# S5 scan chain in two PSUM banks of the product's ring, its steps spread over the whole first product

## The chip, the core and the metric

The kernel runs on one core of a Trainium2 chip, as one program. The metric is the device time of one execution in microseconds (us); lower is better. The engines are called as in the profile: PE (TensorE matmul), DVE (VectorE), ACT (ScalarE), POOL (GpSimd) and SP (SyncE, which here only starts DMAs). SBUF is the working memory of all engines; PSUM is the memory of eight banks that PE writes its results to, and that DVE and ACT can read and write.

## The reference

The whole reference is an S5 layer, an attention layer and a mixed attention and RWKV layer, on 512 positions of 2048 channels. The change lies in the first product of the S5 layer and in the scan beside it; the rest of the program stays as it is.

```python
def s5_ssm(u, a_re, a_im, log_dt, b_re, b_im, c_re, c_im, d_skip):
    """u: (B,S,W) -> Re(C h_t) + D*u_t, h_t = Abar h_{t-1} + Bbar u_t per 16-channel group."""
...
    _, _, h_re, h_im = lax.associative_scan(combine, (a_seq_re, a_seq_im, x_re, x_im), axis=1)
    y = (jnp.einsum('bsgp,gcp->bsgc', h_re, c_re.astype(F32))
         - jnp.einsum('bsgp,gcp->bsgc', h_im, c_im.astype(F32)))
...
def s5_layer(h, g_pre, g_post, w_in, ...):
    xn = rmsnorm(h, g_pre)
    uz = xn @ w_in
    u, z = jnp.split(uz, 2, axis=-1)
    y = s5_ssm(u, a_re, a_im, log_dt, b_re, b_im, c_re, c_im, d_skip)
    y = jax.nn.gelu(y)
    y = y * jax.nn.sigmoid(y @ w_glu.astype(F32) + b_glu.astype(F32))
    y = y.astype(h.dtype) * jax.nn.silu(z)
    return h + rmsnorm(y @ w_out, g_post)
```

## The kernel before, in words

**The first product.** `phase1` computes `xn @ w_in` as 32 tiles of 128 channels by 512 positions, 16 for u and 16 for z, in the order `order1`: five z tiles first (`ZF`), then a u tile every 1.35 tiles (`UR`), and z tiles between and behind them. A tile (`gemm`) is four chunks of 12 matmuls of 128x512, into one bank `acc` of the ring `pq`, which has four PSUM banks. Each chunk calls `tick` once, so the program counts 128 ticks in this product. Its weights come as `raw` by DMA; ACT rounds them to `wh` (L199), and DVE subtracts to get the rest `wl` (L200, both inputs in SBUF). PE can't begin a chunk without its `wh` and `wl`.

**The scan beside it.** The 128 groups of the S5 layer are done in 16 steps j of eight groups. POOL makes the matrices `In` and `Ox` of four groups at a time (`s5_pool`, 32 calls of six operations, L505 to L507) from the power tables `PT` and `Q` and the inputs `bc`. PE makes from them `kb` and the transposes `tb` (`s5_mats`), and ACT copies these out. A finished u tile is scaled on DVE, goes to DRAM (`ud`) and comes back in another order (`U`), and PE multiplies `InT` with `U` into the bank `xb` (`s5_x`). Then comes the chain of the step on DVE: the rotation (`s5_rot`, L609 to L612), the scan along time (`s5_scan`, L618), ACT's copies with halves exchanged (`Gw`), and the rotation back into `H` (`s5_back`, L630 to L632). PE then computes `yb` (`s5_y`, L642 without H, L644 with H), and DVE and ACT apply the gelu (`s5_gelu`, `s5_out`, L652 and L658), whose result goes to DRAM as `y2d`. `s5_phase` makes the rotation tables (L574 to L576 on DVE, every second j) from `e1` and `e8`, which DVE itself computes in `s5_tables` during the first ticks, with the scratch pool `b0`.

**What sets the order.** `later(dt, f)` puts a step dt ticks behind the current tick, and each tick runs what is due; so the program is written as one stream. The framework then schedules that stream by its own estimate of durations and gives each engine a queue. An engine takes its queue strictly in order: a row that waits holds all rows behind it. SP's queue carries the DMAs of `bc`, `dd`, `ud`, `U`, `toep`, `y2d` and `zd`, and waits likewise. Buffers of a ring come free in turn: `tmp` has eight, `In` and `bc` three, `Ox` six, and `sp` (which holds `bc`, `In`, `Ox` and the working tiles) is opened where `b0` ends. The S5 banks `kb`, `tb`, `xb`, `yb` are a second ring `ps` of four.

After the last tile `phase2` begins a product that needs all sixteen `y2d`.

Of the kernel before, what the change touches and what calls it, by code (L numbers as in the profile page):

```python
# [39 lines left out]
ZF, UR = 5, 1.35  # L40
# [109 lines left out]
class Kern:  # L150
# [337 lines left out]
    def s5_pool(self, hb):  # L488

        nc, sp = self.nc, self.sp  # L490
        PT, Q, go = self.PT, self.Q, hb * 4
        bc = sp.tile([128, 4, 4, 16], F32, tag="bc", name="bc", bufs=3)
        nc.sync.dma_start(bc.rearrange("p a g c -> p (a g c)"), self.I["s5bc"][hb])
        B1, B2, C1, C2 = (bc[:, i] for i in range(4))
        e = nc.gpsimd

        def prod(name, tab, X1, X2, n, bufs, kin):

            shp = [128, 4, 16, n] if kin else [128, 4, n, 16]
            ku, cu = (2, 3) if kin else (3, 2)  # L500
            o = sp.tile(shp, F32, tag=name, name=name, bufs=bufs)
            t = sp.tile([128, 4 * 9 * 16], F32, tag="ptmp", name="ptmp", bufs=1)[:, :64 * n]
            t = t.rearrange("p (g k c) -> p g k c", g=4, k=shp[2])
            tr, ti = (tab[:, i, :, go:go + 4].rearrange("p k g -> p g k").unsqueeze(ku).broadcast_to(shp) for i in range(2))
            e.tensor_tensor(o, tr, X1.unsqueeze(cu).broadcast_to(shp), ALU.mult)  # L505
            e.tensor_tensor(t, ti, X2.unsqueeze(cu).broadcast_to(shp), ALU.mult)
            e.tensor_tensor(o, o, t, ALU.subtract)  # L507
            return o

        self.In[hb] = prod("In", Q, B1, B2, 8, 3, True)  # L510
        self.Ox[hb] = prod("Ox", PT, C1, C2, 9, 6, False)
        if hb % 2 == 0:
            d = self.dd[hb // 2] = sp.tile([128, 128], F32, tag="dd", name="dd", bufs=2)
            nc.sync.dma_start(d, self.I["s5dd"][hb // 2])
# [85 lines left out]
    def s5_rot(self, j):  # L600
# [6 lines left out]
        X = self.X[j] = self.tmp("X")  # L607
        m = sp.tile([128, 512], F32, tag="mX", name="mX", bufs=1)
# [3 lines left out]
        v.tensor_sub(X, X, m)  # L612

    def s5_scan(self, j):
        nc = self.nc
        rt = self.rt[j % len(self.rt)]
        Gs, Gw = self.tmp("Gs"), self.tmp("Gw")
        nc.vector.tensor_tensor_scan(Gs, rt.rearrange("p g k -> p (g k)"), self.X.pop(j), 0.0, ALU.mult, ALU.add)  # L618
        nc.scalar.activation(Gw[0:64], Gs[64:128], AF.Copy)
        nc.scalar.activation(Gw[64:128], Gs[0:64], AF.Copy)  # L620
        self.X[j] = Gs, Gw

    def s5_back(self, j):
# [3 lines left out]
        m = sp.tile([128, 512], F32, tag="mX", name="mX", bufs=1)  # L627
# [3 lines left out]
        v.tensor_tensor(m, Gw, Es, ALU.mult)  # L631
        v.tensor_sub(Hf, Hf, m)  # L632
# [87 lines left out]
    def phase1(self):  # L720
        tc, nc, I, v = self.tc, self.nc, self.I, self.nc.vector
        with ExitStack() as ex:
# [17 lines left out]
            for t in self.rt:  # L740
                nc.gpsimd.memset(t, 0.0)
            b0 = tc.tile_pool(name="b0", bufs=1)
# [6 lines left out]
            for i, n in enumerate(self.order1):  # L749
                if i == ZF:  # L750
                    b0.__exit__(None, None, None)
                    self.sp = P(name="sp", bufs=2)

                    for j in range(16):
# [6 lines left out]
                        for dt, f in ((6, self.s5_mats), (7, self.s5_mats2), (10, self.s5_x), (11, self.s5_rot),  # L761
                                      (12, self.s5_scan), (13, self.s5_back), (15, self.s5_y), (16, self.s5_gelu),
                                      (17, self.s5_out)):
                            at(dt, f, j)
                j = n
                acc = self.gemm(xa)
                if n < 16:
                    self.s5_u(j, acc, r)
                else:
                    z = self.tmp("z")  # L770
                    v.tensor_mul(z, acc, r)
                    t = self.tmp("zt")
                    nc.scalar.activation(t, z, AF.Tanh, scale=0.5)
                    self.later(0, self.z_out, n - 16, z, t)
# [977 lines left out]
```

## Time and profile before

| | us |
|---|---|
| median of 3 runs | 3197.53 |
| lowest to highest run | 3194.95 to 3200.65 |
| profiled execution, own time | 3205.11 |
| profiled execution, span | 3203.3 |
| first product: last matmul begins | 565.57 |
| PE busy over the span | 2999.3 |
| DVE busy over the span | 1907.5 |

The rows come from one profiled execution, whose own time lies 1.8 us above its span and 7.6 us above the median of the runs. A time in a row counts from the start of the span. A mean duration contains the time that an operation is held on its engine. A row of the chain or of the waits says who released whom.

### The profile page before, as it was taken

How to read it: one execution, taken by the hardware profiler on the slowest of the kernel's cores; microseconds unless marked ns; L12 is line 12 of the kernel's file. 1: busy time of each engine (PE TensorE's matmuls, PEld its weight loads, DVE VectorE, ACT ScalarE, POOL GpSimd, SP SyncE). 2: the span in 40 equal slices, each digit the busy share in tenths (PEclk: the TensorE clock that was granted, in tenths of full speed). 3: DMA queues.
4: the chain of work that ended last, by engine and by line, in shares of the span. 5: the costliest groups of instructions: out<-in, count | busy, mean ns of one | idle time of the engine just before them, and what ended most of it. 6: DMA issues, size and time to landing. Idle time of an engine off the chain costs nothing.

```text
span 3203.3 us, 46304 instructions
## 1 busy us (share of the span) xinstructions
PE 2999.3 (94%) x17252; PEld 2464.4 (77%) x17252; DVE 1907.5 (60%) x3123; ACT 1143.4 (36%) x2094; POOL 765.4 (24%) x691
## 2 busy tenths in 40 slices
PE   8878789999989999999999997999889999999897
PEld 6766667788879988888888886777679788777685
DVE  9799885543358333555555237487599566645733
ACT  5343443433333222433333334233222354533322
POOL 0688770110020000000000002233288321122200
PEclk9889989999989999999999998999999999999998
DMA  5444444653344333422222335355732433397533
GB/s 156 115 108 115 109 106 121 190 144 102 96 149 132 97 96 96 125 86 87 88 86 83 96 105 176 117 146 149 193 119 87 125 99 96 107 255 215 162 117 109
DMA packets 345027, 397.30 MB, mean 124 GB/s; under 512 B 133809, under 2 KB 182193, under 8 KB 344801
## 3 DMA queue, kind: packets, MB, share of 16 engines
q10 hardware_dynamic: 131328, 237.43, 26.0%
q1 hardware_dynamic: 213472, 156.91, 16.8%
q8 instruction: 136, 2.23, 0.3%
q14 instruction: 91, 0.74, 0.1%
HBM read 325.50 MB, written 59.80 MB: 120 GB/s over the span
## 4 chain that ended last, share of the span: by engine, by line
PE 68%; DVE 15%; issue 4%; DMA 4%; POOL 2%; ACT 2%; SPq 1%; ACTq 0%; DVEq 0%; POOLq 0%
PE acc L226 18%; PE acc L227 18%; PE acc L228 18%; DVE wl L200 3%; PE vb L266 2%; PE vb L267 2%; PE vb L265 2%; PE ob L981 1%; DVE Yi L1197 1%; PE pt L964 1%; DVE w L1196 1%; DVE h L832 1%; DVE Gs L618 1%; SPq L1172 1%; PE xg L1153 1%
## 5 line engine op out<-in xcount | busy, mean ns | idle before, releaser
L226 PE MATMUL acc<-hi,wh 128*128 128x512 f32 x3216 | 1284.6, 400 | 25.7 <-ACT wh L199 9.3
L228 PE MATMUL acc<-hi,wl 128*128 128x512 f32 x3216 | 1279.8, 398 | 10.3 <-DVE wl L200 10.2
L227 PE MATMUL acc<-lo,wh 128*128 128x512 f32 x3216 | 1279.0, 398 | 4.6 <-DVE lo L175 3.9
L200 DVE TENSOR_TENSOR wl<-raw,wh 128x512 fp32r<-128x512 f32 (+2 forms) x912 | 696.3, 767 | 866.2 <-ACT wh L199 855.0
L199 ACT ACTIVATE wh<-raw 128x512 fp32r<-128x512 f32 (+2 forms) x912 | 569.1, 627 | 1420.3 <-PE acc L227 934.6
L226 PEld LDWEIGHTS acc<-hi,wh 128*128 128x128 f32 x3216 | 612.6, 191 | 170.9 <-ACT wh L199 13.0
L228 PEld LDWEIGHTS acc<-hi,wl 128*128 128x128 f32 x3216 | 612.1, 190 | 153.4 <-DVE wl L200 15.5
L227 PEld LDWEIGHTS acc<-lo,wh 128*128 128x128 f32 x3216 | 613.5, 191 | 149.1 <-issue 6.7
L266 PE MATMUL vb<-wl,hi 128*128 128x256 f32 (+2 forms) x768 | 221.3, 289 | 3.3 <-DVE wl L200 3.1
L267 PE MATMUL vb<-wh,lo 128*128 128x256 f32 (+2 forms) x768 | 218.6, 287 | 3.9 <-DVE lo L178 3.8
L265 PE MATMUL vb<-wh,hi 128*128 128x256 f32 (+2 forms) x768 | 217.1, 287 | 2.7 <-DVE us L1548 2.6
L926 POOL TENSOR_TENSOR bm<-bias,cmask 128x512 f32<-128x512 f32 x16 | 21.0, 1315 | 690.1 <-DMA bias<-cumd 484.8
L266 PEld LDWEIGHTS vb<-wl,hi 128*128 128x128 f32 x768 | 148.8, 194 | 5.4 <-DVE wl L200 4.8
L267 PEld LDWEIGHTS vb<-wh,lo 128*128 128x128 f32 x768 | 147.4, 193 | 4.5 <-DVE lo L178 4.4
L265 PEld LDWEIGHTS vb<-wh,hi 128*128 128x128 f32 x768 | 146.9, 193 | 3.7 <-DVE us L1548 2.8
L831 POOL TENSOR_TENSOR y<-y,rstd 128x512 f32<-128x512 f32 x26 | 42.1, 1653 | 412.0 <-ACT rstd L316 412.0
L505 POOL TENSOR_TENSOR In<-Q,bc 128x512 f32<-128x512 f32 x32 | 55.1, 1727 | 132.2 <-DMA bc<-in_s5bc 99.7
L644 PE MATMUL yb<-H,Ox 128*64 128x63 f32 x512 | 42.9, 268 | 40.4 <-DVE H L632 40.4
L802 POOL TENSOR_TENSOR ld<-ld 128x512 f32<-128x512 f32 x16 | 21.8, 1364 | 232.0 <-DMA ld<-zd 114.8
L1196 POOL TENSOR_TENSOR wg<-Yi 128x3 f32<-128x3 f32 (+56 forms) x114 | 63.5, 557 | 21.8 <-DVE Yi L1197 13.8
L644 PEld LDWEIGHTS yb<-H,Ox 128*64 128x64 f32 x512 | 34.1, 179 | 44.2 <-DVE H L632 43.9
L1197 POOL TENSOR_TENSOR Yi<-Yi,wg 128x3 f32<-128x3 f32 (+56 forms) x114 | 62.2, 546 | 8.6
(438 smaller groups left out, 3427.5 us busy)
## 6 DMA issues: line engine op xcount, KB each, us to landing
raw<-in_w ACTq DMA_DIRECT2D x744, 256.0 KB
raw<-in_wk ACTq DMA_DIRECT2D x64, 256.0 KB
raw<-in_wv ACTq DMA_DIRECT2D x56, 256.0 KB
ld<-hd SPq DMA_DIRECT2D x48, 256.0 KB
ld<-y2d SPq DMA_DIRECT2D x32, 256.0 KB
hd<-h SPq DMA_DIRECT2D x32, 256.0 KB
Xd<-X SPq DMA_DIRECT2D x32, 256.0 KB
raw<-in_wd ACTq DMA_DIRECT2D x24, 256.0 KB
```

What stands on the lines that cost most here:

```text
L199: nc.scalar.activation(wh, raw, AF.Copy)
L200: nc.vector.tensor_sub(wl, raw, wh.bitcast(F32))
L226: nc.tensor.matmul(acc, wh[:, sl], hi, start=(kk == 0), stop=False)
L227: nc.tensor.matmul(acc, wh[:, sl], lo, start=False, stop=False)
L228: nc.tensor.matmul(acc, wl[:, sl], hi, start=False, stop=(kk == KT - 1))
L265: nc.tensor.matmul(outs[t], hi[:, tk], wh[:, sl], **st)
L266: nc.tensor.matmul(outs[t], hi[:, tk], wl[:, sl], start=False, stop=False)
L267: nc.tensor.matmul(outs[t], lo[:, tk], wh[:, sl], start=False, stop=(kk == KT - 1 and (W > 256 or t % 2 == 1)))
L505: e.tensor_tensor(o, tr, X1.unsqueeze(cu).broadcast_to(shp), ALU.mult)
L644: nc.tensor.matmul(yb[hs, g * 64 + 1:(g + 1) * 64], Ox[:, hs], H[:, g, 0:63], start=False, stop=True)
L1196: e.tensor_tensor(w, Y[:, a:a + k, t:t + 1].broadcast_to(shp), Y[:, t:t + 1, t + 1:].broadcast_to(shp), ALU.mult)
L1197: e.tensor_tensor(Y[:, a:a + k, t + 1:], Y[:, a:a + k, t + 1:], w, ALU.add)
```

## The change

`Gs` and the product `mX` no longer come from `tmp` and `sp`: `s5_rot` takes two banks of the ring `pq` for them. `X` is still in SBUF, the difference goes into the bank `mX`, the scan reads that bank and writes the bank `Gs`, ACT's two copies go from one bank to the other, and `s5_back` multiplies in place there, with only `H` in SBUF. The tanh of a z tile overwrites the tile's bank `acc`, and `z_out` reads it from there at the next tick; it stands first in that tick. `ZF` and `UR` become 3 and 1.58: the steps start at tick 12 with 6.32 ticks from j to j + 1, where they started at tick 20 with 5.4. Inside a j `s5_x`, `s5_rot`, `s5_scan` and `s5_back` come one tick later, and `s5_y`, `s5_gelu`, `s5_out` two ticks later. `bc`, `In`, `Ox`, `ptmp` and `dd` move to a pool `s5q` that is opened before `b0`, so that their space isn't the space of `b0`; `sp` with the rest is opened behind tile 3.

```diff
--- before.py
+++ after.py
@@ -37,7 +37,7 @@
 
 COLS = {}
 STAT = 10
-ZF, UR = 5, 1.35
+ZF, UR = 3, 1.58
 
 
 def lay(inp):
@@ -487,9 +487,9 @@
 
     def s5_pool(self, hb):
 
-        nc, sp = self.nc, self.sp
+        nc, sq = self.nc, self.s5q
         PT, Q, go = self.PT, self.Q, hb * 4
-        bc = sp.tile([128, 4, 4, 16], F32, tag="bc", name="bc", bufs=3)
+        bc = sq.tile([128, 4, 4, 16], F32, tag="bc", name="bc", bufs=3)
         nc.sync.dma_start(bc.rearrange("p a g c -> p (a g c)"), self.I["s5bc"][hb])
         B1, B2, C1, C2 = (bc[:, i] for i in range(4))
         e = nc.gpsimd
@@ -498,8 +498,8 @@
 
             shp = [128, 4, 16, n] if kin else [128, 4, n, 16]
             ku, cu = (2, 3) if kin else (3, 2)
-            o = sp.tile(shp, F32, tag=name, name=name, bufs=bufs)
-            t = sp.tile([128, 4 * 9 * 16], F32, tag="ptmp", name="ptmp", bufs=1)[:, :64 * n]
+            o = sq.tile(shp, F32, tag=name, name=name, bufs=bufs)
+            t = sq.tile([128, 4 * 9 * 16], F32, tag="ptmp", name="ptmp", bufs=1)[:, :64 * n]
             t = t.rearrange("p (g k c) -> p g k c", g=4, k=shp[2])
             tr, ti = (tab[:, i, :, go:go + 4].rearrange("p k g -> p g k").unsqueeze(ku).broadcast_to(shp) for i in range(2))
             e.tensor_tensor(o, tr, X1.unsqueeze(cu).broadcast_to(shp), ALU.mult)
@@ -510,7 +510,7 @@
         self.In[hb] = prod("In", Q, B1, B2, 8, 3, True)
         self.Ox[hb] = prod("Ox", PT, C1, C2, 9, 6, False)
         if hb % 2 == 0:
-            d = self.dd[hb // 2] = sp.tile([128, 128], F32, tag="dd", name="dd", bufs=2)
+            d = self.dd[hb // 2] = sq.tile([128, 128], F32, tag="dd", name="dd", bufs=2)
             nc.sync.dma_start(d, self.I["s5dd"][hb // 2])
 
     def s5_mats(self, j):
@@ -604,32 +604,30 @@
         Ec, Es = self.E[j]
         rt = self.rt[j % len(self.rt)]
         nc.scalar.activation(rt[:, :, 1:], self.rho[:, j * 8:j * 8 + 8].unsqueeze(2).broadcast_to([128, 8, 63]), AF.Copy)
-        X = self.X[j] = self.tmp("X")
-        m = sp.tile([128, 512], F32, tag="mX", name="mX", bufs=1)
+        Gs, m = self.X[j] = [self.pq.tile([128, 512], F32, tag="g", name=n) for n in ("Gs", "mX")]
+        X = self.tmp("X")
         v.tensor_tensor(X, xb, Ec, ALU.mult)
         v.tensor_tensor(m[0:64], xb[64:128], Es[64:128], ALU.mult)
         v.tensor_tensor(m[64:128], xb[0:64], Es[0:64], ALU.mult)
-        v.tensor_sub(X, X, m)
+        v.tensor_sub(m, X, m)
 
     def s5_scan(self, j):
         nc = self.nc
         rt = self.rt[j % len(self.rt)]
-        Gs, Gw = self.tmp("Gs"), self.tmp("Gw")
-        nc.vector.tensor_tensor_scan(Gs, rt.rearrange("p g k -> p (g k)"), self.X.pop(j), 0.0, ALU.mult, ALU.add)
+        Gs, Gw = self.X[j]
+        nc.vector.tensor_tensor_scan(Gs, rt.rearrange("p g k -> p (g k)"), Gw, 0.0, ALU.mult, ALU.add)
         nc.scalar.activation(Gw[0:64], Gs[64:128], AF.Copy)
         nc.scalar.activation(Gw[64:128], Gs[0:64], AF.Copy)
-        self.X[j] = Gs, Gw
 
     def s5_back(self, j):
         sp, v = self.sp, self.nc.vector
         Gs, Gw = self.X.pop(j)
         Ec, Es = self.E.pop(j)
-        m = sp.tile([128, 512], F32, tag="mX", name="mX", bufs=1)
         H = self.H[j] = sp.tile([128, 8, 64], F32, tag="H", name="H", bufs=1)
         Hf = H.rearrange("p g k -> p (g k)")
         v.tensor_tensor(Hf, Gs, Ec, ALU.mult)
-        v.tensor_tensor(m, Gw, Es, ALU.mult)
-        v.tensor_sub(Hf, Hf, m)
+        v.tensor_tensor(Gw, Gw, Es, ALU.mult)
+        v.tensor_sub(Hf, Hf, Gw)
 
     def s5_y(self, j):
         nc = self.nc
@@ -739,6 +737,7 @@
             self.rt = [self.bp.tile([128, 8, 64], F32, name=f"rt{i}") for i in range(2)]
             for t in self.rt:
                 nc.gpsimd.memset(t, 0.0)
+            self.s5q = P(name="s5q", bufs=2)
             b0 = tc.tile_pool(name="b0", bufs=1)
             self.b0 = b0.__enter__()
             self.s5_base()
@@ -748,8 +747,6 @@
             self.In, self.Ox, self.InT, self.U, self.E, self.H, self.dd, self.kt, self.X, self.Y, self.ph = ({} for _ in range(11))
             for i, n in enumerate(self.order1):
                 if i == ZF:
-                    b0.__exit__(None, None, None)
-                    self.sp = P(name="sp", bufs=2)
 
                     for j in range(16):
                         at = lambda dt, f, *a: self.later(int(4 * UR * j + dt), f, *a)
@@ -758,20 +755,22 @@
                         if j % 2 == 0:
                             for k in range(3):
                                 at(5 + k, self.s5_phase, j // 2, k)
-                        for dt, f in ((6, self.s5_mats), (7, self.s5_mats2), (10, self.s5_x), (11, self.s5_rot),
-                                      (12, self.s5_scan), (13, self.s5_back), (15, self.s5_y), (16, self.s5_gelu),
-                                      (17, self.s5_out)):
+                        for dt, f in ((6, self.s5_mats), (7, self.s5_mats2), (11, self.s5_x), (12, self.s5_rot),
+                                      (13, self.s5_scan), (14, self.s5_back), (17, self.s5_y), (18, self.s5_gelu),
+                                      (19, self.s5_out)):
                             at(dt, f, j)
                 j = n
                 acc = self.gemm(xa)
+                if i == 3:
+                    b0.__exit__(None, None, None)
+                    self.sp = P(name="sp", bufs=2)
                 if n < 16:
                     self.s5_u(j, acc, r)
                 else:
                     z = self.tmp("z")
                     v.tensor_mul(z, acc, r)
-                    t = self.tmp("zt")
-                    nc.scalar.activation(t, z, AF.Tanh, scale=0.5)
-                    self.later(0, self.z_out, n - 16, z, t)
+                    nc.scalar.activation(acc, z, AF.Tanh, scale=0.5)
+                    self.todo.setdefault(self.now, []).insert(0, (self.z_out, (n - 16, z, acc)))
             while self.todo:
                 self.tick()
 
```

Where it moves instructions, the queues read as follows (the numbers in the names are running numbers of the buffers).

DVE, before, chain of j = 2 (`xb_1759` to `H_1899`), with the gelu of the step ahead of it between:

```order
L652 SCALAR_TENSOR_TENSOR q_1796<-q_1796,yb_1726 128x512
L609 TENSOR_TENSOR X_1801<-xb_1759,Ec_1548 128x512
L610 TENSOR_TENSOR mX_1802<-xb_1759,Es_1627 64x512
L611 TENSOR_TENSOR mX_1802<-xb_1759,Es_1627 64x512
L658 SCALAR_TENSOR_TENSOR q_1796<-q_1796,yb_1726 128x512
L612 TENSOR_TENSOR X_1801<-X_1801,mX_1802 128x512
L200 TENSOR_TENSOR wl_2054<-raw_2051,wh_2053 128x512
L618 SCALAR_TENSOR_TENSOR Gs_1848<-rt0_306,X_1801 128x512
L630 TENSOR_TENSOR H_1899<-Gs_1848,Ec_1548 128x512
L558 TENSOR_TENSOR u_1938<-acc_1725,rstd_300 128x512
L631 TENSOR_TENSOR mX_1898<-Gw_1849,Es_1627 128x512
L632 TENSOR_TENSOR H_1899<-H_1899,mX_1898 128x512
```

DVE, after, chain of j = 4 (`xb_2231` to `H_2380`); L628 to L630 are the old L630 to L632, L650 and L656 the old L652 and L658:

```order
L650 SCALAR_TENSOR_TENSOR q_2227<-q_2227,yb_2170 128x512
L609 TENSOR_TENSOR X_2278<-xb_2231,Ec_2006 128x512
L610 TENSOR_TENSOR mX_2277<-xb_2231,Es_2081 64x512
L656 SCALAR_TENSOR_TENSOR q_2227<-q_2227,yb_2170 128x512
L611 TENSOR_TENSOR mX_2277<-xb_2231,Es_2081 64x512
L200 TENSOR_TENSOR wl_2327<-raw_2324,wh_2326 128x512
L612 TENSOR_TENSOR mX_2277<-X_2278,mX_2277 128x512
L618 SCALAR_TENSOR_TENSOR Gs_2276<-rt0_306,mX_2277 128x512
L628 TENSOR_TENSOR H_2380<-Gs_2276,Ec_2006 128x512
L629 TENSOR_TENSOR mX_2277<-mX_2277,Es_2081 128x512
L200 TENSOR_TENSOR wl_2365<-raw_2362,wh_2364 128x512
L630 TENSOR_TENSOR H_2380<-H_2380,mX_2277 128x512
```

The operations are the same; what moved is where `mX` and `Gs` lie. PE has, from the first row of `xb` to the first row of `yb` that reads H, 4.5 ticks of the product in its queue before (mean of 16 steps, 3.2 to 5.6) and 6.04 after (5.0 to 7.0). The first `yb` with H stands behind tick 40.9 before and behind tick 29 after, the last one behind 116.6 and 123.

SP, before, where the first inputs of POOL are loaded (behind all loads of x):

```order
L780 DMA zd3_116<-z_852 128x512
L780 DMA zd4_117<-z_931 128x512
L560 DMA ud0_81<-u_1040 128x512
L493 DMA bc_942<-in_s5bc 128x256
L514 DMA dd_954<-in_s5dd 128x128
L493 DMA bc_992<-in_s5bc 128x256
L562 DMA U_1043<-ud0_81 128x8x64
```

SP, after, the rows from the output of z tile 3 on (three `bc` and two `dd` stand far ahead of them, among the loads of x):

```order
L779 DMA zd3_116<-z_1040 128x512
L560 DMA ud1_82<-u_1147 128x512
L493 DMA bc_1280<-in_s5bc 128x256
L562 DMA U_1150<-ud1_82 128x8x64
L493 DMA bc_1457<-in_s5bc 128x256
```

The first `bc` moved ahead of most of x; the sixth (`bc_1280`) stands behind the output of a z tile, which DVE finishes nine rows behind the last row of the tables.

## Rows read from the trace of the kernel before

**Rows 1.** Stretches: us, busy us (rows) of PE, PEld, DVE, ACT, POOL, PEclk, DMA, GB/s

```profile
155.00:487.00 332.00, 268.41 (x2569) 218.01 (x2567) 289.96 (x254) 149.40 (x271) 259.78 (x161) 0.90 0.44 108
487.00:566.00 79.00, 75.01 (x498) 60.63 (x494) 38.44 (x57) 26.38 (x46) 0.00 (x0) 0.96 0.48 130
566.00:3203.00 2637.00, 2521.42 (x13524) 2080.33 (x13524) 1449.57 (x2553) 901.50 (x1670) 451.76 (x490) 0.97 0.43 125
...
675.00:700.00 25.00, 25.00 (x110) 20.44 (x109) 11.59 (x15) 7.88 (x13) 3.17 (x3) 1.00 0.52 146
```

**Rows 2.** Waits of PE from 155 to 566 us: total us, times, longest us

```profile
PE yb L644 <- DVE H L632: 36.2, 8, 9.6
PE tb L535 <- DVE mX L611: 11.4, 2, 9.6
PE xb L597 <- DMA U<-ud: 11.3, 3, 6.8
PE kb L524 <- POOL Ox L507: 8.2, 5, 2.2
```

**Rows 3.** Groups of DVE, 155 to 487 us: busy us, mean ns | idle before

```profile
L200 DVE TENSOR_TENSOR wl<-raw,wh 128x512 fp32r<-128x512 f32 x64 | 84.3, 1326 | 16.9 <-ACT wh L199 15.8 <-DMA raw<-in_w 1.1
L618 DVE TENSOR_TENSOR_SCAN Gs<-rt,X 128x512 f32<-128x512 f32 x13 | 26.8, 2061 | 0.1
L630 DVE TENSOR_TENSOR H<-Gs,Ec 128x512 f32<-128x512 f32 x13 | 20.5, 1577 | 0.1
L631 DVE TENSOR_TENSOR mX<-Gw,Es 128x512 f32<-128x512 f32 x13 | 20.3, 1564 | 0.2
...
L632 DVE TENSOR_TENSOR H<-H,mX 128x512 f32<-128x512 f32 x13 | 17.9, 1374 | 0.4
L612 DVE TENSOR_TENSOR X<-X,mX 128x512 f32<-128x512 f32 x13 | 16.2, 1247 | 0.0
...
L610 DVE TENSOR_TENSOR mX<-xb,Es 64x512 f32<-64x512 f32 x13 | 9.0, 693 | 0.2
```

**Rows 4.** Groups of DVE, 488 to 566 us, where POOL is idle

```profile
L200 DVE TENSOR_TENSOR wl<-raw,wh 128x512 fp32r<-128x512 f32 x24 | 16.5, 688 | 19.1 <-ACT wh L199 19.1
...
L618 DVE TENSOR_TENSOR_SCAN Gs<-rt,X 128x512 f32<-128x512 f32 x2 | 2.4, 1222 | 0.0
...
L631 DVE TENSOR_TENSOR mX<-Gw,Es 128x512 f32<-128x512 f32 x2 | 1.4, 692 | 0.8 <-ACT Gw L620 0.8
```

**Rows 5.** PE in order of time: start us, us, operation, [idle before <-releaser]

```profile
351.30 0.34 PE L642 MATMUL yb<-U,toep 128*64 128x64 f32 x4
...
353.09 0.29 PE L644 MATMUL yb<-H,Ox 128*64 128x63 f32 x4
360.21 1.98 PE L597 MATMUL xb<-U,InT 128*64 128x64 f32 x32 [6.83 <-DMA U<-ud]
...
445.00 1.15 PE L597 MATMUL xb<-U,InT 128*64 128x64 f32 x32 [0.47 <-DMA U<-ud]
...
447.61 0.48 PE L226 MATMUL acc<-hi,wh 128*128 128x512 f32 x1
```

**Rows 6.** Chain that ended last, around 355 us: start us, us, what

```profile
351.77 3.62 DMA ud<-u
...
355.45 4.62 DMA U<-ud
```

**Rows 7.** DVE and POOL in order of time, end of the tables

```profile
76.33 0.82 DVE L467 TENSOR_SCALAR PT<-PT,cols 128x1152 f32<-128x1152 f32 x1
...
100.09 0.68 DVE L416 TENSOR_TENSOR e<-cm 128x256 f32<-128x256 f32 x1
...
103.46 3.85 POOL L505 TENSOR_TENSOR In<-Q,bc 128x512 f32<-128x512 f32 x1 [99.75 <-DMA bc<-in_s5bc]
```

**Rows 8.** One group of POOL to 487 us: busy us, mean ns | idle before

```profile
L505 POOL TENSOR_TENSOR In<-Q,bc 128x512 f32<-128x512 f32 x32 | 55.1, 1727 | 132.2 <-DMA bc<-in_s5bc 99.7 <-PE tb L535 21.7 <-DMA raw<-in_w 10.7
```

**Rows 9.** Line 1368, beside POOL at times: ns min/median/max

```profile
L1368 DVE TENSOR_TENSOR g2s<-g,g2s x8: 425/518/1372, 2744.9 to 2883.9; 128x256 fp32r<-128x256 f32 x8
```

## The prediction

> **What bounds the kernel now.** I first read the stretches [rows 1] to see where PE, which carries the whole program, has gaps. Behind the first product, from 566 us on, it is busy 2521 of 2637 us at a clock share of 0.97; the order of that part hardly moves, so I leave it at nothing. Where 110 matmuls of the product follow each other without a gap they take 25.00 us, so one takes 0.2273 us and a tick of twelve 2.73 us. From 155 to 566 us PE is busy only 268.4 + 75.0 = 343.4 of 411 us, and up to 487 us the clock share is 0.90. The waits [rows 2] say for whom: 36.2 us for H of the scan chain, 11.4 for the rotation to free a bank, 11.3 for U, 8.2 for POOL, in all 67.1. Then I compared DVE's groups beside POOL [rows 3] with the same lines once POOL has stopped [rows 4]. L200 takes 1.326 us against 0.688, the scan 2.061 against 1.222, L631 1.564 against 0.692: operations with both inputs in SBUF are held while POOL works. L610, which reads one input from PSUM, takes 0.693 us in the same stretch. DVE is busy 290 us for 13 chains, 22.3 us for each, and each takes 332 / 13 = 25.5 us.
>
> What would PE alone need for a step? At full clock the rows of xb, kb and tb stand from 445.00 to 447.61, 2.6 us, and those of yb from 351.30 to about 353.2, 1.9 us [rows 5]: 4.5 us. With 5.4 ticks of 2.73 that makes 19.2 us per step. So DVE with 22.3 us sets the pace, and what it lags stands as a wait for H.
>
> **The chain in PSUM.** Five operations of each chain now read one input from PSUM. If each then takes what it takes without POOL (0.69, the scan 1.22), a chain saves (1.247 - 0.69) + (2.061 - 1.222) + (1.577 - 0.69) + (1.564 - 0.69) + (1.374 - 0.69) = 3.84 us [rows 3, 4]. No row shows DVE writing PSUM, as L612, the scan and L629 now do. Bounds: as cheap as L610 (the whole 3.84), or as dear as now (only L628 and L630 gain, 1.57 us). I take the first, since L610 differs only in where it writes, and nothing in the rows of DVE suggests a price for that; the end costs 2.3 us a step. ACT's copies and the tanh cover themselves as before, since their count is the same. z_out gains likewise, less than 0.5 us a step.
>
> [...]
>
> **The wider pace.** A step gets 6.32 ticks: PE needs 6.32 x 2.73 + 4.5 = 21.8 us. DVE needs 22.3 - 3.8 + 0.92 more weights (1.2) + a little more z (0.3) = 20.0 us. The order of the two turns: PE becomes the pace, by 1.8 us. And between xb and the yb that needs its H, PE's queue holds 6.04 ticks in place of 4.5, which is 4.2 us more of cover; with the shorter chain 8.0 us. The longest wait for H was 9.6, the mean of eight 4.5 [rows 2], so most vanish. What stays are the steps in which the phase tables (six held operations) fall between; I leave 8 us of the 36.2. U has at least three ticks and a yb (10 us) behind its tile in PE's queue; ud and U take 3.62 + 4.62 us [rows 6] and the scaling under one. So 2 of the 11.3 us stay. The banks of `ps` are used as before: 10 of 11.4 stay. POOL: 7, worked out below.
>
> The ring of four banks now also holds Gs and mX. I looked for a product that would take a bank of a chain not yet done: each such product stands in PE's queue behind the yb of that chain, which has waited for the same H. So I cost it at nothing; if that cover were gone, a product would wait for up to a whole chain.
>
> **The start.** POOL now has its buffers early and waits only for the power tables, whose last row ends at 77.15 us, not for `bc` until 103.46 [rows 7]. In DVE's queue two weights and a z row less stand ahead, so about 75: 28 us earlier. But between 77 and 100.8 us DVE computes e1 and e8, 36 small operations and nine weights, all with two inputs in SBUF, until now without POOL. No row shows these beside POOL. Bounds: nothing added, or the 0.9 us that L631 loses on the mean (1.564 - 0.692) for each of the 45, 40 us. The nearest row is L1368, 256 elements: 425 ns at best, median 518, up to 1372 [rows 9]. POOL stops by itself: its 25th operation needs the sixth `bc`, which in SP's queue stands behind the output of a z tile, nine DVE rows behind the tables. 24 operations of some 1.55 us (1.73 in [rows 8], less where DVE is quick) last 37 us, and hold about as many operations of DVE, 24 x 0.9 = 22 us. The tables then end at 123, z_out at 127; eleven more rows, two of them held, and ACT's copies take 12 us to H of step 0 at 139, and yb, still at the lower clock, ends at 143. Range of the start: 121 to 161.
>
> [...] L1368's median of 518 against 425 ns speaks against a hold each time.
>
> POOL goes on at 130 and has 15 operations, 23 us, to the second half of the matrices of step 2, at 153; PE is there at 149. With some small waits: 7 us. Two `dd` and three `bc` ahead of x add 0.5 MB to the loading; PE's first 30 us could lose 0 to 2 us; I take 1.
>
> **The sum.** From the end of the first yb, PE's queue holds 128 - 29 = 99 ticks (270.3 us), 15 yb (28.5) and 15 times xb, 14 times kb and tb (37.6): 336 us. Before, the same point was reached at 155 us with 87.1 ticks left: 304 us. 155 + 304 = 459, but the product ended at 566. [...] After: waits 8 + 2 + 10 + 7 = 27, clock in proportion 16, and 7 for waits that the rigid order makes anew, together 50. 143 + 1 + 336 + 50 = 530, against 566: 36 us less. The profiled execution's 3205.1 becomes 3169, and the median of the runs, 7.6 us lower, 3161. The tail behind yb moves from 11.4 to 5 ticks before the end; gelu, store, load and split of the last y2d (about 11 us, by the transfers of [rows 6] and four operations of 0.7) then still lie beside 13.7 us of product and the next tile's first chunks. If that cover were gone, it would cost up to 10 us.
>
> **Rivals.** (A) DVE goes on pacing at half. If the PSUM writers are held as now, DVE needs 22.3 - 1.6 + 1.5 = 22.2 us a step against PE's 21.8. Then half of what I took off stays: a loss of 78 in place of 50, end 558, 3189. For it: [rows 3] show weights and phase tables still held; against: L610. (B) Slower. The waits for H come not from held operations but from the circle of the queues: PE frees a weight buffer, ACT rounds, DVE subtracts, and only then does the chain behind it in DVE's queue move. For it: DVE idled 15.8 us behind ACT's wh [rows 3], and weights still stand within each chain. Then the 107 us are lost as before, behind a later start: 143 + 1 + 336 + 107 = 587, 21 more, 3218. It decides from a loss of 86 us on. Against it: 290 of 332 us DVE was busy. (C) More. The start costs only 130 and all waits for H vanish (loss 30): 497, 3128; I count down to 3138.
>
> **How the numbers follow.** Forecast 0.62, A 0.18, B 0.10, C 0.10. The range goes from 3138 to 3200 and leaves out B and part of C; within it lie the bounds of the PSUM writers (35 us, between forecast and A) and of the start (121 to 161, so -22 to +18). A measurement of this kernel can tell about 0.2% (6.4 us) from no change. Faster by more: the forecast, C and half of A, 0.81; within: the other half of A, 0.09; slower: 0.10.
>
> **What would show it.** L612, L618 and L628 to L630 at 0.69 and 1.22 us beside POOL: the saving holds; at 1.5: A. POOL's first operation near 75 us with a gap near 112 to 130, first yb near 143: the start holds. Waits for H under 10 us and a clock share over 0.94 from 155 us on: the pace has gone to PE; H still over 25: B. The product ending at 530. I would be wrong if the tables are held much longer, if waits for banks of the ring appear before the products, or if the later part moves by more than 5 us.

## The result, and the profile after

The changed kernel takes 3156.8 us (median; 3154.8 to 3161.8), the kernel before, run beside it, 3196.2: a ratio of 0.988, 95% interval 0.986 to 0.990, 39 us less. A second series gave 3155.0 us and 0.987 (0.986 to 0.989). The forecast was 3161.

The profiled execution took 3161.8 us with a span of 3158.7. Its stretches, in the columns of [rows 1], the last one from the end of the first product on:

```profile
0.00:75.00 75.00, 59.98 (x229) 44.51 (x230) 68.24 (x174) 39.36 (x64) 3.52 (x10) 0.98 0.53 163
75.00:103.00 28.00, 18.60 (x70) 14.50 (x69) 27.76 (x28) 2.53 (x4) 22.54 (x15) 0.83 0.13 39
103.00:155.00 52.00, 32.30 (x313) 25.38 (x311) 45.27 (x55) 22.26 (x41) 35.93 (x24) 0.80 0.37 100
155.00:487.00 332.00, 314.92 (x2902) 257.12 (x2903) 240.84 (x291) 163.61 (x298) 231.45 (x154) 0.98 0.52 133
...
521.00:3158.00 2637.00, 2519.55 (x13524) 2080.86 (x13524) 1451.02 (x2553) 901.87 (x1670) 450.21 (x490) 0.97 0.42 125
```

From 155 to 487 us PE is busy 315 us where it was 268, at a clock share of 0.98 where it was 0.90 [rows 1]. The product ends at 520.6 us (before 566.0), and what follows takes 2638 us as before (2637). The whole gain lies in the first product. Its start has become worse: in the first 155 us PE was busy 134.5 us before, and is 110.9 now. For before, the three stretches to 155 us read:

```profile
0.00:75.00 75.00, 64.90 (x259) 49.41 (x260) 68.02 (x176) 41.52 (x68) 3.19 (x9) 1.00 0.52 154
75.00:103.00 28.00, 28.00 (x123) 22.92 (x122) 26.14 (x57) 6.33 (x11) 0.00 (x0) 1.00 0.44 132
103.00:155.00 52.00, 41.59 (x296) 33.11 (x297) 35.38 (x31) 18.26 (x32) 50.66 (x32) 0.85 0.44 118
```

The waits of PE up to the product's end, after (to be held against [rows 2], which begin at 155 us):

```profile
PE xb L597 <- issue: 15.1, 1, 15.1
PE acc L226 <- ACT hi L177: 10.2, 3, 7.0
PE acc L228 <- DVE wl L200: 9.4, 2, 5.2
PE kb L524 <- POOL Ox L507: 7.2, 1, 7.2
PE tb L535 <- DVE q L656: 5.6, 2, 2.9
PE xb L597 <- DMA U<-ud: 5.1, 4, 1.8
PE acc L226 <- DVE u L558: 4.2, 1, 4.2
PE tb L535 <- DVE mX L611: 3.2, 1, 3.2
PE yb L642 <- DVE H L630: 0.6, 2, 0.3
```

H cost 36.2 us and costs 0.6. The first three lines and that of u lie ahead of 155 us; the wait called "issue" is taken up in experiment 4. VectorE's groups from 155 to 480 us, beside POOL, answer to [rows 3]:

```profile
L200 DVE TENSOR_TENSOR wl<-raw,wh 128x512 fp32r<-128x512 f32 x85 | 87.4, 1030 | 44.3 <-ACT wh L199 42.6 <-PE yb L642 1.5
L618 DVE TENSOR_TENSOR_SCAN Gs<-rt,mX 128x512 f32<-128x512 f32 x14 | 17.1, 1218 | 0.1
...
L612 DVE TENSOR_TENSOR mX<-X,mX 128x512 f32<-128x512 f32 x14 | 9.7, 696 | 0.5
L629 DVE TENSOR_TENSOR mX<-mX,Es 128x512 f32<-128x512 f32 x14 | 9.6, 688 | 0.0
L628 DVE TENSOR_TENSOR H<-Gs,Ec 128x512 f32<-128x512 f32 x14 | 9.6, 686 | 9.9 <-ACT mX L620 9.8
```

The scan fell from 2061 to 1218 ns, the others of the chain from between 1247 and 1577 to some 690. L612, the scan and L629 write PSUM too and are not held: 696, 1218 and 688 ns, where L610, which writes SBUF, took 693 [rows 3], and the scan and L631 without POOL 1222 and 692 [rows 4].

### The profile page after: what moved, and what is told of

It is laid out like the page before. It is cut to its first block, busy times and chain, and to the rows that moved or that the text cites. A ratio compares the mean times of both kernels' runs of the same rounds, so it can differ in the third digit from the quotient of the medians.

```text
span 3158.7 us, 46260 instructions
## 1 busy us (share of the span) xinstructions
PE 2979.0 (94%) x17252; PEld 2449.7 (78%) x17252; DVE 1850.8 (59%) x3123; ACT 1141.0 (36%) x2094; POOL 743.7 (24%) x691
## 4 chain that ended last, share of the span: by engine, by line
PE 70%; DVE 12%; DMA 5%; POOL 4%; issue 3%; ACT 2%; SPq 2%; ACTq 0%; DVEq 0%; POOLq 0%
PE acc L227 19%; PE acc L226 19%; PE acc L228 19%; DVE wl L200 3%; PE vb L266 2%; PE vb L267 2%; PE vb L265 2%; POOL wg L1195 1%; POOL Yi L1196 1%; PE ob L980 1%; PE pt L963 1%; DMA raw<-in_w 1%; DVE w L1195 1%; DVE Yi L1196 1%; DVE h L831 1%
## 5 line engine op out<-in xcount | busy, mean ns | idle before, releaser
L200 DVE TENSOR_TENSOR wl<-raw,wh 128x512 fp32r<-128x512 f32 (+2 forms) x912 | 688.8, 758 | 873.0 <-ACT wh L199 855.0
L226 PEld LDWEIGHTS acc<-hi,wh 128*128 128x128 f32 x3216 | 612.3, 190 | 173.5 <-ACT hi L177 12.3
L505 POOL TENSOR_TENSOR Ox<-PT,bc 128x576 f32<-128x576 f32 x32 | 44.7, 1402 | 118.0 <-DVE PT L467 71.0
L1195 POOL TENSOR_TENSOR wg<-Yi 128x3 f32<-128x3 f32 (+56 forms) x114 | 63.0, 552 | 22.7 <-DVE Yi L1196 14.3
L1196 DVE TENSOR_TENSOR Yi<-Yi,w 128x504 f32<-128x504 f32 (+29 forms) x99 | 58.3, 613 | 7.4 <-POOL Yi L1196 7.0
L286 DVE TENSOR_TENSOR acc<-acc,sq 128x512 f32<-128x512 f32 x87 | 59.7, 686 | 1.8
```

Of the source, the lines that this page charges most:

```text
L200: nc.vector.tensor_sub(wl, raw, wh.bitcast(F32))
L226: nc.tensor.matmul(acc, wh[:, sl], hi, start=(kk == 0), stop=False)
L286: nc.vector.tensor_add(s.acc, s.acc, q)
L1195: e.tensor_tensor(w, Y[:, a:a + k, t:t + 1].broadcast_to(shp), Y[:, t:t + 1, t + 1:].broadcast_to(shp), ALU.mult)
L1196: e.tensor_tensor(Y[:, a:a + k, t + 1:], Y[:, a:a + k, t + 1:], w, ALU.add)
```

## One sum for all runs

To compare the experiments I use the prediction's own sum: the end of the first yb, what PE's queue still holds behind it at the prices of the prediction, and the rest up to the end of the product, called the loss. It is worked out from one profiled execution of each kernel (us), so a few us of difference between two rows say little:

| kernel | ticks done, first yb ends | still to do | sum without loss | loss | product ends |
|---|---|---|---|---|---|
| before | 40.9, 155.7 | 303.7 | 459.4 | 106.6 | 566.0 |
| changed | 29.0, 144.6 | 336.2 | 480.8 | 39.8 | 520.6 |
| changed, chain in SBUF | 29.1, 142.1 | 336.0 | 478.1 | 84.6 | 562.7 |
| before, chain in PSUM | 35.0, 148.2 | 319.9 | 468.1 | 49.4 | 517.4 |
| changed, old pace | 35.0, 153.8 | 319.9 | 473.7 | 43.0 | 516.6 |
| changed, tables first | 29.0, 140.1 | 336.2 | 476.3 | 37.2 | 513.6 |
| before, PSUM chain, scan from SBUF | 35.0, 149.2 | 319.9 | 469.1 | 60.4 | 529.4 |
| before, POOL emptied | 39.8, 146.0 | 306.7 | 452.7 | 14.3 | 467.0 |
| late steps | 38.0, 152.2 | 311.7 | 463.9 | 39.0 | 502.9 |

A low first number is not a good start: a step that begins early leaves more product behind it.

## Experiments

**1. The chain back in SBUF.** Is it the chain's place or the pace?

```diff
-        Gs, m = self.X[j] = [self.pq.tile([128, 512], F32, tag="g", name=n) for n in ("Gs", "mX")]
-        X = self.tmp("X")
+        X = self.X[j] = self.tmp("X")
+        m = sp.tile([128, 512], F32, tag="mX", name="mX", bufs=1)
...
-        Gs, Gw = self.X[j]
+        Gs, Gw = self.tmp("Gs"), self.tmp("Gw")
```

> The changed kernel with the chain's four tiles (X, mX, Gs, Gw) back in SBUF; the pace, the tables' own buffers and the gate's tanh stay as changed. My theory: operations with both inputs in SBUF are held beside POOL, so the chain grows back by some 3.8 us a step, from about 20 to about 24 us on DVE against PE's 21.8, and DVE sets the pace again. The scan should read 2.0 us and more, L631 and L633 about 1.5, and waits for H of over 15 us should return; the first product ends 20 to 45 us later, the time is 3177 to 3202. Rival, that the wider pace did it: the slack of about six ticks covers the longer chain, H waits stay under 5 us, and the time stays under 3167.

Measured: 3198.9 us, ratio 1.0003 (0.9994 to 1.0012). All of the gain is gone; the new pace, the tables' buffers and the gate's tanh in PSUM give nothing without the chain. The order of the queues hardly moved with the edit: from xb to yb PE has 5.9 ticks (6.04 in the changed kernel), and the first yb stands behind tick 29 in both. The groups of VectorE, 155 to 480 us, are held as before (the chain's last row is L632 here, not the L633 of the expectation):

```profile
L200 DVE TENSOR_TENSOR wl<-raw,wh 128x512 fp32r<-128x512 f32 x73 | 92.8, 1277 | 28.2 <-ACT wh L199 24.8 <-DMA ud<-u 1.1 <-DMA bc<-in_s5bc 1.1
L618 DVE TENSOR_TENSOR_SCAN Gs<-rt,X 128x512 f32<-128x512 f32 x12 | 25.4, 2114 | 0.0
L630 DVE TENSOR_TENSOR H<-Gs,Ec 128x512 f32<-128x512 f32 x12 | 19.5, 1624 | 0.1
...
L631 DVE TENSOR_TENSOR mX<-Gw,Es 128x512 f32<-128x512 f32 x12 | 17.8, 1482 | 0.8 <-DVE Ss L576 0.5 <-ACT Gw L620 0.2
```

One thing came out as the rival said: the wait for H stays small. PE's waits from 155 us to the product's end:

```profile
PE xb L597 <- DMA U<-ud: 17.1, 4, 7.0
PE acc L228 <- DVE wl L200: 11.8, 6, 3.1
PE tb L535 <- DVE mX L611: 9.6, 3, 4.3
PE yb L644 <- DVE H L632: 3.6, 2, 3.0
```

The six ticks of slack do cover the chain. But VectorE is then late with weights, with u and with the banks (the longest wait for U ends at 178.8 us; VectorE scaled that u at 169.2, right behind the held rows of a chain). The loss shrinks by 22 us only, and the earlier first step costs 19 (table, 478.1 against 459.4).

**2. The chain in PSUM alone.** The kernel before with that one edit (the inverse of the diff above).

> The kernel before with one part of the change alone: the chain in two PSUM banks of the ring. Pace, buffers of the tables and the gate as before, so POOL starts near 103 us as before. My theory: 3.8 us a step less on DVE (22.3 to about 18.5, under PE's 19.2), waits for H fall from 36 to under 15 us, the first product ends 25 to 45 us earlier than 566, the time is 3152 to 3172. Rival, that the wider pace did it: with the old slack of 4.5 ticks and the old pace the waits for H stay over 25 us, and the time stays within 10 us of the kernel before.

Measured: 3153.0 us, ratio 0.9853 (0.9835 to 0.987). One part of the change carries all of it. From 155 us on:

```profile
PE yb L642 <- DVE H L630: 11.0, 5, 3.7
```

```profile
L618 DVE TENSOR_TENSOR_SCAN Gs<-rt,mX 128x512 f32<-128x512 f32 x15 | 18.3, 1218 | 0.0
```

H waits fall from 36.2 to 11.0 us, the loss from 106.6 to 49.4. POOL starts at 103.62 us, as before. The framework moved the queues a little with this edit (4.9 ticks from xb to yb in place of 4.5, the first yb behind tick 35.0 in place of 40.9); experiments 1 and 6 change where operands lie and leave the order nearly or wholly as it was. The changed kernel has 10 us less loss than this, and a start that is 13 us worse (table); the two cancel.

**3. The old pace in the changed kernel.**

```diff
-ZF, UR = 3, 1.58
+ZF, UR = 5, 1.35
...
-                        for dt, f in ((6, self.s5_mats), (7, self.s5_mats2), (11, self.s5_x), (12, self.s5_rot),
+                        for dt, f in ((6, self.s5_mats), (7, self.s5_mats2), (10, self.s5_x), (11, self.s5_rot),
...
-                if i == 3:
+                if i == 4:
```

> The changed kernel with the old pace: the steps begin with the sixth tile and follow each other after 5.4 ticks in place of 6.32, x to y as near as before. The chain and the gate stay in PSUM, the tables keep their own buffers (POOL may start near 75 us). My theory: PE needs 19.2 us a step, DVE about 19, so neither covers the other well; some 5 to 15 us of waits for H return, the tail of the product without steps is filled by z tiles, and the time is 3150 to 3172. Rival, that the wider pace did it: waits for H over 25 us, and the time is over 3180.

Measured: 3154.0 us, 0.986 (0.9846 to 0.9875); H waits are 12.3 us from 75 us on (11.0 in experiment 2). With the chain in PSUM the pace makes no difference to the time that these runs show.

**4. Tables first.** What made the start bad? In the changed kernel POOL begins at 74.67 us, while VectorE still computes the tables. VectorE in order of time there:

```profile
73.78 0.81 DVE L467 TENSOR_SCALAR PT<-PT,cols 128x1152 f32<-128x1152 f32 x1
...
75.71 1.78 DVE L467 TENSOR_SCALAR PT<-PT,cols 128x1152 f32<-128x1152 f32 x1
...
83.74 1.39 DVE L415 TENSOR_TENSOR s<-cm 128x64 f32<-128x64 f32 x1
...
87.81 0.28 DVE L414 TENSOR_TENSOR cm<-s 128x128 f32<-128x128 f32 x1
88.13 1.12 DVE L415 TENSOR_TENSOR s<-cm 128x64 f32<-128x64 f32 x1
89.17 0.21 DVE L416 TENSOR_TENSOR s<-cm 128x64 f32<-128x64 f32 x1
...
104.01 0.22 DVE L415 TENSOR_TENSOR s<-cm 128x64 f32<-128x64 f32 x1
...
118.98 1.63 DVE L416 TENSOR_TENSOR e<-cm 128x256 f32<-128x256 f32 x1
```

An operation of 0.22 us takes 1.1 to 1.4 while POOL is at work. From 75.7 to 98.4 us, 15 of 18 operations of VectorE are held, beside 15 of POOL; from 105.6 to 120.6, 9 of 9 beside 9. POOL pauses twice:

```profile
105.61 1.50 POOL L505 TENSOR_TENSOR In<-Q,bc 128x512 f32<-128x512 f32 x1 [7.60 <-PE tb L535]
...
132.88 1.23 POOL L505 TENSOR_TENSOR Ox<-PT,bc 128x576 f32<-128x576 f32 x1 [12.75 <-DMA bc<-in_s5bc]
```

The tables end at 120.6 us. ScalarE then copies InT, whose buffer lies where the tables were, and PE starts xb with a wait of 15.1 us:

```profile
120.70 1.08 ACT L553 ACTIVATE InT<-tb 128x512 f32<-128x512 f32 x2 [10.36 <-DVE e L416]
```

The experiment puts POOL's two prerequisites, q2 and the signs, last:

```diff
-        return [first, p1, q1, p2, q2, sign, ea, eb]
+        return [first, p1, q1, p2, ea, eb, q2, sign]
...
-                self.later(1 + 2 * i, f)
+                self.later(1 + 3 * i // 2, f)
```

> The changed kernel with the power tables' steps in another order: the two large multiplications into the tables' last powers come before the steps that the other table and the signs need, three steps in two ticks. POOL can then start only when the tables are done, and nothing of the tables is computed beside POOL. If the hold of the tables' 36 small operations beside POOL is what put the end of the tables at 120.6 us (theory 1), they end near 100 us, the wait of 15 us before the first xb goes, and the first yb starts 8 to 20 us earlier than 142.7; the time is 3137 to 3150. If what POOL has to deliver bounds the start (theory 2: it starts 25 us later and needs about 36 us for the first matrices), PE waits for POOL's Ox or In at the first steps instead, for 10 us and more, and the time is within 6 us of the changed kernel.

Measured: 3157.2 us, 0.9867 (0.9853 to 0.9881), as the changed kernel. The tables end at 97.4 us and the 15 us before xb are gone, but POOL, which now starts at 94.55 us, is late instead:

```profile
PE kb L524 <- POOL Ox L507: 20.3, 2, 19.0
PE tb L535 <- POOL In L507: 6.2, 2, 4.1
```

That is the second theory; the first yb ends 4.5 us earlier. Either the tables or POOL's first matrices are late for a step that stands at tick 24 in PE's queue.

**5. The gate's tanh back in SBUF.**

```diff
-                    nc.scalar.activation(acc, z, AF.Tanh, scale=0.5)
-                    self.todo.setdefault(self.now, []).insert(0, (self.z_out, (n - 16, z, acc)))
+                    t = self.tmp("zt")
+                    nc.scalar.activation(t, z, AF.Tanh, scale=0.5)
+                    self.later(0, self.z_out, n - 16, z, t)
```

> The changed kernel with the tanh of the gate written to SBUF again, so that z's last operation on VectorE reads two inputs from SBUF. Where POOL is at work this one should take 1.2 to 1.6 us in place of 0.69, some 0.5 us a step, 7 us of VectorE in all. Since PE now sets the pace and the waits for H are 0.6 us in sum, my theory says that nearly nothing of it reaches the end: the first product ends 0 to 4 us later, the time is within 5 us of the changed kernel's 3156.8. Rival, that VectorE still bounds the steps: 7 us and more, over 3163.

Measured: 3164.1 us where the kernel before, run beside it, took 3202.3, ratio 0.9887 (0.9864 to 0.9911): not distinguishable from the changed kernel's 0.988 and 0.987, though the time itself lies over the 3163 of the rival. z's last operation is held as expected (1215 ns; 686 in PSUM), and PE's wait for the bank of the fifth tile fell from 4.2 to 2.3 us. In the profiled execution the product ends at 526.9 us, 6.2 later than in the changed kernel where 0 to 4 were expected; 2.5 of it stand before the end of the first yb. One such execution doesn't decide between the theory and a small price of the held operation.

**6. What must lie in PSUM, an input or any end?** The chain in PSUM as in experiment 2, but the scan reads its data from SBUF and writes PSUM.

```diff
-        v.tensor_sub(m, X, m)
+        v.tensor_sub(X, X, m)
+        self.Xs = X
...
-        nc.vector.tensor_tensor_scan(Gs, rt.rearrange("p g k -> p (g k)"), Gw, 0.0, ALU.mult, ALU.add)
+        nc.vector.tensor_tensor_scan(Gs, rt.rearrange("p g k -> p (g k)"), self.Xs, 0.0, ALU.mult, ALU.add)
```

> The kernel before with the chain in PSUM, but the rotated X is written to SBUF, so that the scan reads two inputs from SBUF and writes its result to PSUM; all else of the chain stays in PSUM. Theory 1, that two inputs from SBUF are what is held beside POOL, wherever the result goes: the scan takes 2.0 us and more as before, the others of the chain 0.69. Theory 2, that an operation which has any end in PSUM is free: the scan takes 1.22 us. In time 0.9 us a step lie on VectorE, which has room there: 3150 to 3165 in both cases, so the duration is the answer.

The groups, 155 to 480 us:

```profile
L619 DVE TENSOR_TENSOR_SCAN Gs<-rt,X 128x512 f32<-128x512 f32 x14 | 30.1, 2148 | 0.4
...
L612 DVE TENSOR_TENSOR X<-X,mX 128x512 f32<-128x512 f32 x14 | 9.5, 678 | 0.1
```

The inputs decide: with both in SBUF the scan is held although it writes PSUM (2148 ns, 1218 in experiment 2), and L612, which reads PSUM and writes SBUF, is not (678 ns). The order of the queues is that of experiment 2 (from xb to yb the same ticks in all 16 steps). The time was not as expected: 3169.8 us, 0.9905 (0.9881 to 0.9929), 17 us more than experiment 2 by the ratios, 12 by the end of the product. 0.93 us more in the mean of the 14 scans shown, 13 us, went to the end nearly whole. VectorE was not full: 254 of 332 us, by the stretches of this run and of experiment 2:

```profile
155.00:487.00 332.00, 299.74 (x2830) 241.71 (x2829) 253.58 (x285) 159.07 (x289) 255.44 (x159) 0.95 0.50 125
155.00:487.00 332.00, 308.09 (x2929) 248.69 (x2928) 246.74 (x294) 162.88 (x297) 241.88 (x159) 0.97 0.51 129
```

Two things grew: the waits for H, 11.0 to 15.1 us, and POOL, whose 159 operations in the stretch took 255.4 us in place of 241.9. My reading, which no run tests, is that with a slack of some five ticks the chain's length, not VectorE's sum, still set the step; which of the two paths carried how much of it I cannot tell.

**7. POOL emptied.** The suspected cause itself, in the kernel before. The kernel leaves out POOL's work and the loads of `bc` from the second step on, and `In` and `Ox` keep two buffers each:

```diff
+        if hb > 1:
+            self.In[hb], self.Ox[hb] = self.keep[hb % 2]
...
+            return
```

> The kernel before, its chain in SBUF as it was, with nearly all of POOL's work taken away: POOL computes the matrices of the first step alone, and all later steps use these, so the output is wrong. If POOL's operations are what lengthens those of VectorE (theory 1), all lines of the chain take 0.69 us and the scan 1.22 from the second step on, VectorE needs under 18 us a step, the waits for H fall under 15 us, and the first product ends 35 to 60 us earlier without any tile in PSUM: 3135 to 3165. Rival, that the waits came from the order of the queues or from PSUM being quicker in itself: the chain stays long or the waits stay, and the time is over 3180.

Measured: 3106.9 us, 0.9701 (0.967 to 0.9732); the product ends at 467 us, and PE waits 1.5 us in all from 155 us on. The stretch and the groups, chain in SBUF:

```profile
155.00:487.00 332.00, 326.52 (x3004) 265.35 (x3003) 215.09 (x321) 180.29 (x319) 1.73 (x1) 0.99 0.55 144
```

```profile
L200 DVE TENSOR_TENSOR wl<-raw,wh 128x512 fp32r<-128x512 f32 x88 | 60.2, 687 | 51.1 <-ACT wh L199 50.0 <-DMA U<-ud 0.7
L625 DVE TENSOR_TENSOR_SCAN Gs<-rt,X 128x512 f32<-128x512 f32 x14 | 17.1, 1218 | 0.1
...
L638 DVE TENSOR_TENSOR mX<-Gw,Es 128x512 f32<-128x512 f32 x15 | 10.3, 690 | 4.1 <-ACT Gw L627 3.6 <-DVE Ss L583 0.5
```

So POOL's work, with what hangs on it, stood behind 92 of the 107 us of loss, at the old pace and nearly in the old order (4.8 ticks from xb to yb, the first yb behind tick 39.8). The hold is not all that the edit takes away: PE's waits for POOL's matrices go too (8.2 us before [rows 2]), and so do the loads of `bc`, at which SP's queue stood 31.7 us from 155 us on. Experiment 2 parts them: there SP stood at `bc` for 47.7 us, and yet the waits for U fell from 11.3 us to 0.3 and the loss by 57. The other 35 of the 92 are not parted by a run. The gain was larger than I had expected (3135 to 3165); the weights go free with the chain (687 ns, where the changed kernel has 1030), and I take that for the reason.

**8 to 11. A better version.** Its aim is a good start with a small loss: the tables first, the old pace, all steps behind POOL two ticks later, and six ticks from x to y. Against the run with the old pace:

```diff
+        return [first, p1, q1, p2, ea, eb, q2, sign]
...
-                        for dt, f in ((6, self.s5_mats), (7, self.s5_mats2), (10, self.s5_x), (11, self.s5_rot),
-                                      (12, self.s5_scan), (13, self.s5_back), (15, self.s5_y), (16, self.s5_gelu),
-                                      (17, self.s5_out)):
+                        for dt, f in ((8, self.s5_mats), (9, self.s5_mats2), (12, self.s5_x), (13, self.s5_rot),
+                                      (14, self.s5_scan), (15, self.s5_back), (18, self.s5_y), (19, self.s5_gelu),
+                                      (20, self.s5_out)):
```

> A version that takes up what the runs showed: chain and gate in PSUM, tables with buffers of their own, the large steps of the power tables first so that POOL starts near 95 us, the old pace of 5.4 ticks, but all steps behind POOL two ticks later (first matrices at tick 29, so that products stand in PE's queue where the run with the tables first waited 19 us for POOL), and six ticks from x to y. If PE's waits at the start are the loss left (theory 1), the 25 us of waits for POOL and wl go and the first product ends near 500: 3135 to 3148. If POOL's 19 us a step bound the product from its start on (theory 2), waits for Ox and In appear at later steps and the time stays at 3150 to 3158.

Measured: 3138.9 us, 0.9812 (0.9786 to 0.9838). The start gains 17 us against the changed kernel (463.9 against 480.8), the loss stays at 39. As the first theory says, PE's waits for POOL, 26.5 us in experiment 4, are 3.5; but several parts were changed at once, and the runs don't say which carries the gain. Then the changed kernel once more beside two variants: the gate in SBUF (the diff of experiment 5), and on top of it the matrices one tick later (8 and 9 become 9 and 10).

> The changed kernel as it is, on the same chip as the two versions after it. Expected: 0.988 of the kernel before, as found (0.986 to 0.990).

> The version with late steps, with the gate's tanh in SBUF again, so that a product's bank is given back by the first read of z instead of after the tanh and z's last operation. In the version with the gate in PSUM, PE waits 5.9 us for z before its fifth tile; with the gate in SBUF 2.35 us in an earlier run. Theory, that the held bank costs more than the held z operation: this wait falls to under 3 us, z's last operation takes 1.2 to 1.5 us beside POOL, and the time is 0 to 5 us less than that of the version with the gate in PSUM, relative to the kernel before 0.978 to 0.981. Rival: the longer z operations cost 5 us and more, over 0.983.

> The version before (late steps, gate in SBUF) with the two halves of the matrices one tick later in each step, behind the gelu of the step that holds the bank they take. The waits for q of 12.8 us in the version with late steps come from that bank. Theory, that the order in the queue sets them: they fall under 6 us, and the time falls by 3 to 7 us against the version before this one. Rival, that VectorE's gelu operations are late whatever the order: the waits for q stay at 10 us or return as waits for the matrices' transfers to SBUF before x, and the time stays within 3 us.

The changed kernel took 3155.0 us, ratio 0.9872 (0.9859 to 0.9886). With late steps and the gate in SBUF: 3137.9 us, 0.9816 (0.9803 to 0.983), 17 us less on the same chip, the intervals apart. Waits of PE in that version, up to 570 us:

```profile
PE tb L535 <- DVE q L656: 10.3, 3, 5.2
...
PE acc L228 <- DVE wl L200: 7.6, 5, 3.9
PE kb L524 <- POOL Ox L507: 5.3, 3, 3.3
```

The gate's place makes no difference again (0.9816 beside 0.9812, just above the 0.978 to 0.981 expected), though the bank did go free sooner (2.4 us of wait for z; 5.9 with the gate in PSUM) and z's last operation took 1125 ns. With later matrices: 3141.3 us, 0.9827 (0.9814 to 0.9841), no gain; the waits for q fell from 10.3 to 7.9 us only, which is neither of the two theories.

## Why the prediction was right, step by step

- **What bounded the kernel: shown.** Held operations of VectorE, not the circle of queues (rival B): the chain's place alone moves the time from 1.0003 to 0.988 at the same pace and in nearly the same order (experiment 1), the place of the scan's data alone moves it by 17 us in the same order (6), and without POOL nearly all waits go (7).
- **The chain, 3.84 us a step: shown.** L612 696, L629 688, L628 686, L630 677, the scan 1218 ns, each as without POOL [rows 4]. Rival A, held writers, did not come: 0 of its price. (The 35 us for the bounds of the writers, 2.3 in each of 15 steps, don't fit between the forecast and A, which lie 28 apart.)
- An input from PSUM cost nothing that the rows show: L629 took 688 ns with one, and the same product with both inputs in SBUF took 690 in the run with POOL emptied (L638 there).
- **VectorE per step was mis-sized.** Forecast 20.0 us. A step took 24.1 us from the first yb to the last, so 240.84 us in 332 / 24.1 = 13.8 steps are 17.5. Weights took 1.03 us in place of 1.33. That POOL worked less doesn't explain it: in experiment 2 it was busy for 242 of 282 us up to its last operation (before: 260 of 324), and the weights beside it took 1.07 us (before 1.34). Fewer of the weights beside POOL were held, 41 of 77 in the changed kernel where it was 42 of 61, and a held one took a median of 1.35 us in place of 1.72. Why freeing the chain does this, no run shows.
- **The wider pace: the step that failed.** I let it give more than half of the cover that removes the waits for H (4.2 of 8.0 us). It does cover H, 0.6 us where I left 8. But to spread the steps it begins them at tile 3, and the worse start takes back what is gained behind it: with the tables' buffers and the gate, but without the PSUM chain, 19 of 22 us (time 1.0003), and 13 against 10 with the chain. The table parts these 13 and 10: buffers and gate cost 5.6 us of start and give 6.4 of loss (changed with the old pace, against the PSUM chain alone), the pace costs 7.1 and gives 3.2. The chain should have carried the whole gain, and the pace nothing.
- **The start: right in sum, not in its parts.** The first yb ends at 144.6 us (forecast 143). The tables end at 120.6 (123): that each of POOL's operations there, 24, holds one of VectorE was right. POOL's pause for bc came as told, but from 120 to 132.9 us, not from 112 to 130, and ahead of it came one from 98.0 to 105.6 that I had not seen: In's ring waited for PE's transposes. The 15.1 us before xb, a buffer that the tables still held, were not in the steps either, so that 144.6 lies so near to 143 is partly luck. Up to 75 us PE was busy 5 us less than before, where I took 1: it waited 14.4 us for hi and for a bank, before 9.4.
- The upper end of the range for the start, 161 us, did not come: POOL had 24 operations until 120.1 us, and of VectorE's 44 they held 24, not all; 17 ran free in its pause from 98.0 to 105.6 us.
- **POOL at step 2: right.** Forecast were 7 us, of which 4 for one wait that ends at 153; there was one wait of 7.2 us, and it ended at 157.6.
- **The loss: 39.8 us against 50.** Waits behind the first yb are 7.2 + 5.6 + 5.1 + 3.2 + 0.6 = 21.7 us (27 forecast: H 0.6 for 8, the banks 8.8 for 10, POOL 7.2 for 7, U 5.1 for 2), the clock and the rest 18 (16); the 7 us kept for new waits were not needed there. No run shows the 16 us for the clock, nor a clock loss in proportion to the waits; what the runs showed is a clock share of 0.50 behind two waits (before 360.2 to 364.3 us, changed kernel 123.6 to 127.0), a share of 0.90 from 155 to 487 us before and 0.98 after, and a loss outside the waits of 106.6 - 67.1 = 39.5 us before and 18 after. 10 us less loss, 1 us of start: 520.6 against 530. Of these 9 us, 1 was lost behind the product and 1 between the span and the execution's own time, and the profiled execution lay 5.0 us above the median and not 7.6; so the time came out 4 us under the forecast.
- **Tail and later part at nothing: right.** 2638 us against 2637.

The time thus came out right by one step, the chain; what pace, buffers and gate gave behind the first yb, the start took back. My own lines showed it, since 143 + 1 + 336 is 480 and before it was 459: 21 us given away at the start. I did not ask what the chain would give without the rest.

## What to carry to other kernels

Where VectorE works beside a busy POOL, look for operations with both inputs in SBUF, and give one input of each of a critical chain a PSUM bank; here the scan went from 2.06 to 1.22 us by it, and the output lay in either memory (L612 writing PSUM 696 ns, writing SBUF 678). Slack ahead of one wait was worth nothing while VectorE behind it was late for other consumers too (experiment 1: the waits for H at 3.6 us, the ratio at 1.0003): test it alone before it is counted. An earlier start of a side task is priced by the work left when it becomes due, not by its clock time (the first yb ends 11 us earlier, and the sum without loss is 21 us longer).

## What the runs showed of the hardware beyond that

- In the operations of three lengths below, the hold adds up to 1.2 us: 0.22 us becomes 1.1 to 1.4 (128x64, changed kernel), a weight's 0.69 becomes 0.8 to 1.9 (same), the scan's 1.22 becomes 2.2 to 2.4 (kernel before). POOL's own operations from 155 to 487 us took 1.6 us in the mean (259.78 / 161, kernel before).
- An operation with one tensor in SBUF and a column as its scalar (L467) was held too, 0.81 to 1.78 us (rows of experiment 4).
- The hold seems to go both ways: with the scan's inputs in SBUF, POOL's operations took 255.4 / 159 = 1.61 us in place of 241.9 / 159 = 1.52 (experiments 6 and 2, one profiled execution each).
